# Batches of a group taken eight apart in a batched matrix product, with one store per group

## The chip, the cores and the metric

The kernel runs on one core of a Trainium2 chip. The core has five engines that take instructions on their own: PE (TensorE, matrix products), DVE (VectorE), ACT (ScalarE), POOL (GpSimd) and SP (SyncE, which here only waits and issues transfers). Data moves between the memory HBM and the on-chip buffer SBUF by DMA, over 16 DMA engines; matrix products land in PSUM, from which ACT and DVE copy them to SBUF. The time is the device time of one execution in microseconds; the kernel before takes 132.02 us (median of 3 runs, 131.93 to 132.05).

## The reference

```python
batch, dim_i, dim_j, dim_k = 32, 256, 512, 384
x: (batch, dim_i, dim_j) float32;  y: (batch, dim_j, dim_k) float32
out = np.einsum('bij,bjk->bik', x, y).astype(np.float32)
```

There are 32 independent products of a 256 x 512 by a 512 x 384 matrix. A batch of x has 512 KiB, of y 768 KiB, of out 384 KiB; 41.94 MB are read and 12.58 MB written.

## The kernel before

The 32 batches are worked on in `N` = 8 groups of `Q` = 4. The four batches of a group lie on the 128 partitions of SBUF side by side, 32 partitions (`PQ`) each. A partition holds 8 whole rows of x of its batch (16 KiB, one run in HBM), 16 rows of y (24 KiB, one run) and at the end 8 rows of out (12 KiB, one run). In the kernel before, a group is made of four neighbouring batches, so that partition p of the tile and the p-th run of the group in HBM go on evenly through all 128.

The four PE row groups of 32 each compute one of the four batches at the same time (`product`). The work on a group goes through the engines so:

- SP issues the loads into `x_sb` and `y_sb`, float32, two buffers each (`load_x`, `load_y`).
- POOL rounds them to float16, into `x_r` (two halves of a group, `NE`) and `y_r` (`round_x`, `round_y`; two or four pieces of y).
- DVE transposes x in blocks of 32 into `xt_sb` (`transpose_x`).
- PE accumulates over the 16 steps `t` into eight PSUM banks, one for each batch and half.
- ACT and DVE copy PSUM to `o_sb` (`collect`), which has room for all eight groups, so that no store has to be done before a later group is computed.
- SP issues the stores.

The order is written by hand, with semaphores. SP issues y(0), x(0), x(1), y(1) first. Then, for each group n from 2 on, x(n) follows when POOL has cast both halves of x(n-2), whose buffer it takes, and y(n) when the first half of x(n-1) has been cast, which POOL does after y(n-2). The stores stand behind all loads on SP: one of the groups 0 to 4 once group 5 is well on its way (`JOINED` = 5), one of 5 and 6 once group 7 is, and one of group 7 when ACT and DVE have copied it. A transfer adds 16 to its semaphore when it is done, and whoever uses the tile waits for 16.

Of the lines that the change touches, the source of a load and the target of a store are these:

```python
src = y[n * Q : (n + 1) * Q].rearrange("g (q t) k -> (g q) t k", t=T)
groups = out[first * Q : last * Q].rearrange("(n g) (s f) k -> (g s) n f k", g=Q, s=PQ)
```

## Time and profile before

| | |
|---|---|
| median of 3 runs | 132.02 us |
| the profiled execution, its own time | 132.13 us |
| its span, from the first to the last instruction | 130.8 us |
| bytes by the load and store queue | 54.53 MB |
| busy: PE / DVE / ACT / POOL | 47% / 63% / 64% / 57% of the span |
| mean granted TensorE clock | 0.823 |

The page cuts the span into 40 equal slices and gives for each the busy share in tenths (9 is 90% or more); the DMA row is the mean over the 16 DMA engines. A row of a queue has its packets, its megabytes and the time that the packets took as a share of 16 engines' span. A row of DMA issues has the kind of transfer, how many, the size of one, and the median time from issue to landing. In the table by stage each row is a stretch of the span, with the busy time and count of each engine, the granted clock, the DMA share and the GB/s. A row of waits says who waited for whom, how long in all and how often. L-numbers are lines of the kernel.

### The profile page before, as it was taken

Reading aid. Unit: us, or ns where it says so; the run is one execution under the profiler, and the core shown is the slowest. Engines: PE = TensorE matmul, PEld = TensorE weight load, DVE = VectorE, ACT = ScalarE, POOL = GpSimd, SP = SyncE. Lnnn points to the kernel's source line nnn. Section 1 sums busy time; section 2 is a strip of 40 time slices with the busy share of each in tenths; the row PEclk is TensorE's granted clock in tenths of the full one; section 3 lists DMA queues with packets and bytes.
Section 4 is the critical chain, followed back from the end, with each engine's and each line's share of the span. In section 5 each row is a group of like instructions: output and inputs, shape, how many; then the busy total and the mean of one; then the engine's idle time right before and its main releaser. Section 6 shows DMA issues by size and latency. Waiting matters only on the chain. (4 is left out here: it accounts for less than half of the span.)

```text
span 130.8 us, 3199 instructions
## 1 busy us (share of the span) xinstructions
PE 61.4 (47%) x1024; PEld 46.7 (36%) x1024; DVE 82.7 (63%) x144; ACT 84.1 (64%) x178; POOL 74.2 (57%) x42
## 2 busy tenths in 40 slices
PE   0000009910992589089329905980975499100000
PEld 0000009800991566046129604970953236000000
DVE  0000036899379999985997997599999957920000
ACT  0400000599659989993998899399999957994000
POOL 0006991199929965992899459758973970000000
PEclk9999999995589689977986985599599959965555
DMA  5999999999999999999999999999999999999995
GB/s 120 451 396 441 421 431 451 443 408 428 451 413 421 438 443 401 436 436 443 423 458 398 443 408 466 398 418 436 463 398 408 427 438 425 436 428 421 425 440 248
DMA packets 3379, 54.55 MB, mean 417 GB/s; under 512 B 304, under 2 KB 304, under 8 KB 304
## 3 DMA queue, kind: packets, MB, share of 16 engines
q1 hardware_dynamic: 3376, 54.53, 98.1%
q14 instruction: 3, 0.02, 0.0%
HBM read 41.94 MB, written 12.58 MB: 417 GB/s over the span
## 5 line engine op out<-in xcount | busy, mean ns | idle before, releaser
L165 ACT COPY o_sb<-o_ps (+1 forms) x176 | 82.6, 469 | 31.7 <-PE o_ps L217 29.6
L217 PE MATMUL o_ps<-y_r,xt_sb 32*128 32x384 f16 x1024 | 61.4, 384 | 50.4 <-PEq L214 49.5
L217 PEld LDWEIGHTS o_ps<-y_r,xt_sb 32*128 32x128 f16 x1024 | 46.7, 107 | 64.6 <-issue 56.8
L156 DVE STREAM_TRANSPOSE xt_sb<-x_r 128x256 f32<-128x256 f32 x64 | 38.1, 626 | 30.9 <-POOL x_r L126 18.4
L136 POOL CAST y_r<-y_sb 128x1536 f16<-128x1536 f32 (+1 forms) x22 | 44.3, 2049 | 15.8 <-DMA y_sb<-in_y_dram 15.3
L165 DVE COPY o_sb<-o_ps 32x384 f32 (+1 forms) x80 | 44.6, 557 | 1.6
L126 POOL CAST x_r<-x_sb 128x2048 f16<-128x2048 f32 x16 | 30.2, 1893 | 16.8 <-DVE o_sb L165 12.1
L202 ACT ACT_TABLE_LOAD x1 | 1.3, 1283 | 3.4 <-PEq L78 3.4
L265 POOL MEMSET const-float32-0.0<- 128x1 f32 x1 | 0.1, 98 | 0.2 <-issue 0.2
L202 ACT COPY spare<-const-float32-0.0 1x1 f32<-1x1 f32 x1 | 0.2, 190 | 0.0
L265 POOL MEMSET const-bfloat16-1.0<- 128x1 bf16 x1 | 0.1, 101 | 0.0
L265 POOL MEMSET const-uint8-127<- 128x1 uint8 x1 | 0.1, 101 | 0.0
L265 POOL MEMSET const-float32-1.0<- 128x1 f32 x1 | 0.1, 98 | 0.0
## 6 DMA issues: line engine op xcount, KB each, us to landing
y_sb<-in_y_dram SPq DMA_DIRECT2D x8, 3072.0 KB, 16.8
x_sb<-in_x_dram SPq DMA_DIRECT2D x8, 2048.0 KB, 17.0
out_dram<-o_sb SPq DMA_DIRECT2D x1, 7680.0 KB, 33.9
out_dram<-o_sb SPq DMA_DIRECT2D x1, 3072.0 KB, 17.3
out_dram<-o_sb SPq DMA_DIRECT2D x1, 1536.0 KB, 11.5
```

What stands on the lines that cost most here:

```text
L126: po.tensor_copy(x_r[:, e], x_sb[n % 2][:, e * H : (e + 1) * H]).then_inc(s_cast, 1)
L136: ins = po.tensor_copy(y_r[:, s], y_sb[n % 2][:, s])
L156: v.transpose(xt_w[:, w], words[:, e, w]).then_inc(s_xt, 1)
L165: ins = copy(o_sb[g * PQ : (g + 1) * PQ, n, e, h], o_ps[h * PQ : (h + 1) * PQ, e * Q + g, :K],)
L202: a_.copy(spare, nc.const_aps.tensor(0.0, [1, 1], F32))
L217: return te.add_instruction(mybir.InstMatmult(name=nc.get_next_instruction_name(), start_tensor_calc=start, stop_tensor_calc=stop, tile_si ...
L265: nc = _bacc.Bacc("TRN2", target_bir_lowering=False, num_devices=1)
```

## The change

Group n is now made of the batches n, n + 8, n + 16 and n + 24 (`x[n::N]`), where it had 4n to 4n + 3. The four batches of a group lie 8 batches apart in HBM: 4 MiB in x, 6 MiB in y, 3 MiB in out. Within a batch the 32 runs still follow each other without a gap. The pattern of the DRAM side of each transfer thus has the counts 4, 32 and a run, where it had 128 and a run; the SBUF side has 128 partitions as before. In place of three stores there are eight, one for each group, with the same pattern; they are issued at the same three points. The final wait is for the eight.

```diff
     def load_x(n):
-        src = x[n * Q : (n + 1) * Q].rearrange("g (p r) j -> (g p) r j", r=R)
+        src = x[n::N].rearrange("g (p r) j -> g p (r j)", r=R)
         return nc.sync.dma_start(out=x_sb[n % 2], in_=src).then_inc(s_x[n], 16)
 
     def load_y(n):
-        src = y[n * Q : (n + 1) * Q].rearrange("g (q t) k -> (g q) t k", t=T)
+        src = y[n::N].rearrange("g (q t) k -> g q (t k)", t=T)
         return nc.sync.dma_start(out=y_sb[n % 2], in_=src).then_inc(s_y[n], 16)
...
-    def store(first, last):
-        groups = out[first * Q : last * Q].rearrange("(n g) (s f) k -> (g s) n f k", g=Q, s=PQ)
-        src = o_sb[:, first:last].rearrange("p n e h k -> p n (e h) k")
-        sp.dma_start(out=groups, in_=src).then_inc(s_out, 16)
+    def store(n):
+        dst = out[n::N].rearrange("g (s f) k -> g s (f k)", s=PQ)
+        src = o_sb[:, n].rearrange("p e h k -> p (e h k)")
+        sp.dma_start(out=dst, in_=src).then_inc(s_out, 16)
...
-    sp.wait_ge(s_pe, chunk_done(JOINED, NE - 1, 0))
-    store(0, JOINED)
-    sp.wait_ge(s_pe, chunk_done(N - 1, NE - 1, 0))
-    store(JOINED, N - 1)
-    sp.wait_ge(s_act, NE)
-    sp.wait_ge(s_dve, NE)
-    store(N - 1, N)
+    for n in range(N):
+        if n == 0:
+            sp.wait_ge(s_pe, chunk_done(JOINED, NE - 1, 0))
+        elif n == JOINED:
+            sp.wait_ge(s_pe, chunk_done(N - 1, NE - 1, 0))
+        elif n == N - 1:
+            sp.wait_ge(s_act, NE)
+            sp.wait_ge(s_dve, NE)
+        store(n)
     sp.sem_inc(s_sp, 1)
-    sp.wait_op(s_out, 16 * 3, "sem-ge").then_inc(s_out, -16 * 3)
+    sp.wait_op(s_out, 16 * N, "sem-ge").then_inc(s_out, -16 * N)
```

## The prediction

> **What bounds the kernel now.** I read the page's slices first, then its queues, then the table by stage, the issues with their landings, and the chain of waits. The first lines are from the page of the kernel before.

> ```profile
> span 130.8 us, 3199 instructions
> ...
> DMA  5999999999999999999999999999999999999995
> ...
> DMA packets 3379, 54.55 MB, mean 417 GB/s; under 512 B 304, under 2 KB 304, under 8 KB 304
> ...
> q1 hardware_dynamic: 3376, 54.53, 98.1%
> ...
> HBM read 41.94 MB, written 12.58 MB: 417 GB/s over the span
> ...
> ACT 8%; PE 2%; issue 0%
> ```

> The DMA digits stand at 9 in every slice but the two ends, and the one queue fills all 16 DMA engines for 98.1% of the span. The chain of waits carries only 8% of ACT and 2% of PE, because it is followed through compute instructions and loses the trail where a transfer is what is late. So the bound is the movement of 54.53 MB, and no compute engine. The stages say it with rates; the columns that matter are the last two, the share of the 16 DMA engines and the GB/s.

> ```profile
> core 0: us, PE busy (x) PEld busy (x) DVE busy (x) ACT busy (x) POOL busy (x), PEclk, DMA share, GB/s
> 0.00:2.50 2.50, 0.00 (x0) 0.00 (x0) 0.00 (x0) 0.00 (x0) 0.20 (x4) 1.00 0.62 138
> 2.50:20.00 17.50, 0.62 (x7) 0.52 (x11) 1.56 (x3) 1.47 (x2) 9.13 (x6) 1.00 0.98 418
> 20.00:60.00 40.00, 26.04 (x439) 20.85 (x434) 33.32 (x59) 30.99 (x66) 29.47 (x14) 0.84 1.01 431
> 60.00:90.00 30.00, 18.75 (x332) 14.98 (x324) 25.65 (x46) 25.30 (x54) 21.29 (x10) 0.82 1.00 427
> 90.00:107.00 17.00, 11.24 (x176) 7.77 (x176) 15.30 (x27) 16.01 (x35) 14.04 (x10) 0.84 1.00 426
> 107.00:119.60 12.60, 4.74 (x88) 2.62 (x80) 6.86 (x12) 10.32 (x22) 0.03 (x1) 0.77 1.00 427
> 119.60:128.00 8.40, 0.00 (x0) 0.00 (x0) 0.00 (x0) 0.00 (x0) 0.00 (x0) 0.50 1.01 432
> 128.00:130.80 2.80, 0.00 (x0) 0.00 (x0) 0.00 (x0) 0.00 (x0) 0.00 (x0) 0.50 0.51 215
> ```

> From 20 us on, loads alone, loads beside stores and stores alone all run at 426 to 432 GB/s with every DMA engine busy. One DMA engine thus moves 427 / 16 = 26.7 GB/s, whichever way the bytes go. The bytes at that rate are 54.53 / 0.427 = 127.7 us; the other 3.1 us of the span are the start before the first bytes and the last landing. The profiled execution took 132.13 us, 1.33 beyond its span, and 0.11 above the median of 132.02; the sum below is made against 132.13.

> How a transfer is spread over the 16 engines can be read from the small packets: 304 of 3379 are under 512 B. The program has 8 loads of y, 8 of x and 3 stores (the issue rows below), and 304 / 19 = 16: one small packet from each of 16 engines for each transfer, its report to the semaphore. In all 19 transfers the outermost count of the pattern is 128, on the DRAM side as on the SBUF side.

> ```profile
> y_sb<-in_y_dram SPq DMA_DIRECT2D x8, 3072.0 KB, 16.8
> x_sb<-in_x_dram SPq DMA_DIRECT2D x8, 2048.0 KB, 17.0
> out_dram<-o_sb SPq DMA_DIRECT2D x1, 7680.0 KB, 33.9
> out_dram<-o_sb SPq DMA_DIRECT2D x1, 3072.0 KB, 17.3
> out_dram<-o_sb SPq DMA_DIRECT2D x1, 1536.0 KB, 11.5
> ```

> **The change part by part.** *Bytes and rows.* No byte is added or removed, and the contiguous runs are as long as before: 24 KB per partition for y, 16 KB for x, 12 KB for out. PE, DVE, ACT and POOL keep every instruction and every wait; only which batch sits in which partitions differs.

> *The pattern of the loads (the edit that decides).* Four neighbouring batches are one even walk: partition 32 follows partition 31 by the same step in DRAM, so 4 batches of 32 rows are one count of 128. With batches eight apart the step from row 31 to row 32 is another one, and the DRAM side has the counts 4, 32 and a run; the SBUF side keeps 128. Nothing in the trace of before shows a transfer with such a pattern, so its spread is bounded: 16 engines, if the hardware divides the 128 partitions as it does now, and 4, if it divides the outermost count, whose 4 entries can make no more than 4 shares. All rows at hand have 128 outermost, so they fit both ends. I take 4: a share has to be a plain pattern on both sides, and cutting the outermost count is the only cut that leaves each share one walk of 32 rows on both. [...]

> What 4 engines cost: an engine at 26.7 GB/s is taken to keep its rate, since it has kept it in all stages above (418 GB/s, with 0.98 of the engines, at the worst after 2.5 us). Then 4 x 26.7 = 106.8 GB/s, and 54.53 MB take 510.8 us instead of 127.7. With the same 3.1 us at the ends the span is 513.9, and with 1.3 beyond it the time is 515 us. At the 431 GB/s of the second long stage it would be 54.53 / 107.8 + 4.4 = 510; at the 418 of the first, 526.

> *The eight stores.* Each store has the same 4 x 32 pattern on the DRAM side and is in the sum above. Five issues are added on SP's queue.

> ```profile
> L96 SPq DMA_DIRECT2D out_dram<-o_sb x3: 345/390/403, 85.9 to 119.3; - x3
> L73 SPq DMA_DIRECT2D y_sb<-in_y_dram x8: 327/328/531, 0.7 to 84.1; - x8
> ```

> At 390 ns they are 2.0 us of SP. Groups 0 to 4 are stored at the one point where the first large store stood, and group 6 goes right behind group 5 at the point of the second, so no store waits for something new. They lie beside queued transfers; uncovered they would cost the 2.0 us. Whether the new pattern takes SP longer to issue is not to be seen in this trace: at the 531 ns of the slowest issue, against 328, all 24 issues would take 5 us more, also beside transfers.

> *Does the queue ever run dry?* With 107 GB/s a load of y lasts 3.146 / 0.107 = 29 us, a load of x 20 us, a group 49 us. The timeline of SP and of POOL shows how quickly the next issue follows.

> ```profile
> 20.27 0.33 SPq L69 DMA_DIRECT2D x_sb<-in_x_dram  x1
> ...
> 84.11 0.33 SPq L73 DMA_DIRECT2D y_sb<-in_y_dram  x1
> 85.85 33.76 SPq L96 DMA_DIRECT2D out_dram<-o_sb  x3
> ```

> ```profile
> 10.87 5.69 POOL L136 CAST y_r<-y_sb 128x1536 f16<-128x1536 f32 x4 [10.43 <-DMA y_sb<-in_y_dram]
> 16.51 3.73 POOL L126 CAST x_r<-x_sb 128x2048 f16<-128x2048 f32 x2
> ...
> 101.33 5.70 POOL L136 CAST y_r<-y_sb 128x1536 f16<-128x1536 f32 x4 [2.18 <-DMA y_sb<-in_y_dram]
> ```

> The load x(2) follows the last cast of x(0) at once (16.51 + 3.73 = 20.24, issued at 20.27). In the changed kernel, when x(0) has landed, x(1) and y(1) are still queued, 49 us of work against some 4 us of casts; later a buffer comes free with at least the 20 us of an x behind it. At the end, y(7) is in at 101.3 and the last store is issued at 119.3: 18 us of compute. Stores 0 to 4, queued behind y(7), cover it with 5 x 1.573 / 0.107 = 74 us. So the compute, which takes some 12 us a group, hides wholly, its waits on loads grow, and the sum stays at **515 us**.

> **The rivals.** *A: two engines share a way into SBUF.* Cut by batch, engine 0 writes partitions 0 to 31, engine 1 partitions 32 to 63, and so on, in the same order and nearly at the same time. If partitions 32 apart have one entrance of the width of one engine, each pair moves 26.7 GB/s together: 54.53 / 0.0534 = 1021, plus 4.4, 1026 us in full step, and less as one engine gets ahead; from a lead of one entrance on, nothing. The stages of before speak neither for nor against it: there 16 engines ran at once without loss, but between them they also covered all 128 partitions evenly. [...]

> *B: part of that, or the far-apart rows.* The four shares walk DRAM 4 MiB apart in x, 6 in y, 3 in out (8 batches each). If the x loads alone fell to half their rate, 16.8 MB would take 157 us more: 672. Against it speaks that only a quarter of the 427 GB/s is asked of HBM. [...] A pair in step for a part of the run ends here too, 560 to 900 us.

> *C: not slower.* The spread follows the 128 SBUF partitions, and all 16 engines stay at work. The time is then the same 127.7 us of bytes and 4.4 us around, 132.1; it hangs on the split alone. A gain of more than 0.3 us has no place to come from: the last store and its 11.5 us to landing stay.

> **How the numbers follow.** Forecast, four engines at full rate: 0.46, own range 507 to 545. A, mostly in step, 900 to 1030: 0.34. B, 560 to 900: 0.13. C: 0.07. The predicted time is 515. To leave out no more than 2 in 10 the range must take in A: 507 to 1030, which leaves out C and little else. Faster by over 0.2% is 0.03 (the sunny half of C), within 0.2% is 0.03, slower 0.94; 0.2% is about what a measurement of this kernel can tell from no change.

> **What would show it.** The row is from the waits of before.

> ```profile
> POOL y_r L136 <- DMA y_sb<-in_y_dram: 15.3, 5, 10.4
> ```

> Small packets: 24 transfers with 4 each are 96 under 512 B, against 384 if 16 engines report. The queue's share of 16 engines falls to about 25% and the rate to 107 GB/s; under A the rate is down to half of that with the share still near 25%, since a slowed engine is busy longer. The first load of y lands after some 31 us (29 of bytes and 2 of start), or some 60 under A. POOL's waits for y grow from 15.3 us in all to over a hundred. The prediction is wrong if the share stays near 98%, if the rate lies well under 107 GB/s, or if there are slices in which the queue is empty.

## The result, and the profile after

The changed kernel takes 545.41 us (median of 6 runs, 539.61 to 549.49) beside 131.99 us for the kernel before. The ratio is 4.1116, with a 95% interval of 4.0967 to 4.1266; it leaves out the two longest runs, 549.49 and 547.76, which count as slow because they lie more than 1.5% above the shortest. The forecast was 515 us with a range of 507 to 1030; the move is of the size that was forecast, and some 30 us are unexplained by the likeliest case.

The first lines are from the page of the changed kernel; the profiled execution is the longest one, 549.49 us.

```profile
span 548.1 us, 3204 instructions
...
DMA  2222222222222222222222222222222222222221
GB/s 50 56 59 64 77 96 108 91 88 103 107 113 108 105 105 108 109 108 108 108 109 108 108 106 109 110 108 105 106 105 109 106 108 108 108 108 108 108 108 69
DMA packets 3171, 54.55 MB, mean 100 GB/s; under 512 B 96, under 2 KB 96, under 8 KB 96
...
q1 hardware_dynamic: 3168, 54.53, 24.8%
```

The small packets are 96, which is 24 transfers with 4 reports each; the queue fills 24.8% of 16 engines, which is four engines without a pause. The DMA digit is 2 in all slices but the last: the queue did not run dry. But the GB/s row does not stand at 107 from the start. It begins at 50 and needs some six slices of 13.7 us to get there, with a second dip behind. By the row, 7.0 MB have moved after seven slices, and y(0), x(0) and x(1) are 7.34 MB together: the dip falls on the beginning of y(1). Why the rate drops again there was not tried. The table by stage of the same kernel puts numbers to it; the last two columns are the DMA share and the GB/s.

```profile
0.00:30.00 30.00, 0.00 (x0) 0.00 (x0) 0.00 (x0) 0.00 (x0) 0.20 (x4) 1.00 0.24 53
30.00:60.00 30.00, 0.00 (x0) 0.00 (x0) 0.00 (x0) 1.47 (x2) 2.23 (x2) 1.00 0.25 64
60.00:100.00 40.00, 7.38 (x128) 6.00 (x128) 7.57 (x13) 8.93 (x20) 7.19 (x5) 0.95 0.25 98
100.00:150.00 50.00, 8.49 (x128) 7.95 (x128) 9.75 (x17) 4.38 (x10) 9.17 (x4) 0.53 0.25 97
150.00:200.00 50.00, 8.09 (x128) 7.10 (x128) 10.93 (x20) 11.68 (x26) 9.17 (x4) 0.59 0.25 107
...
480.00:540.00 60.00, 0.00 (x0) 0.00 (x0) 0.00 (x0) 0.00 (x0) 0.00 (x0) 0.50 0.25 107
540.00:548.10 8.10, 0.00 (x0) 0.00 (x0) 0.00 (x0) 0.00 (x0) 0.00 (x0) 0.50 0.11 46
```

In the first 60 us the four engines are as busy as later (0.24 and 0.25) and move half to three fifths as much (53 and 64 GB/s). Against 107 GB/s the five stretches that fall short lose 15.1, 12.1, 3.4, 4.7 and, at the end, 4.6 us (each its length times the missing share of 107): 40 us. At 107 GB/s the bytes take 510 us, and 510 + 40 = 550 accounts for the span of 548. The last loss is that of the end: the DMA share falls to 0.11, as it would if the four engines, some us apart by then, do not end together.

Whom that hits first is seen in the timeline of SP and in the waits of the changed kernel.

```profile
0.73 0.71 SPq L73 DMA_DIRECT2D y_sb<-in_y_dram  x1
1.51 1.13 SPq L69 DMA_DIRECT2D x_sb<-in_x_dram  x2
2.68 48.37 SPq L73 DMA_DIRECT2D y_sb<-in_y_dram  x1
87.24 0.53 SPq L69 DMA_DIRECT2D x_sb<-in_x_dram  x1
104.97 0.53 SPq L73 DMA_DIRECT2D y_sb<-in_y_dram  x1
106.81 24.26 SPq L69 DMA_DIRECT2D x_sb<-in_x_dram  x1
```

```profile
POOL y_r L138 <- DMA y_sb<-in_y_dram: 109.9, 3, 57.3
...
ACT L204 <- PEq L78: 52.2, 1, 52.2
```

POOL waited 57.3 us for the first load of y. The issue of the fourth load held SP for 48.37 us, where most others took 0.5 to 0.7: that was not foreseen, and the start barrier at L78 waited with it (52.2 us on ACT). It was not the only one: the issues of x(3), x(5), x(6) and x(7), each behind loads that were still queued, held SP for 18.65 to 24.26 us. The DMA share of 0.25 beside them says that these holds cost nothing.

### The profile page after: what moved, and what is told of

Read it like the earlier page. It is cut to its first block, busy times and chain, and to the rows that moved or that the text cites. A ratio compares the mean times of both kernels' runs of the same rounds, so it can differ in the third digit from the quotient of the medians.

```text
span 548.1 us, 3204 instructions
## 1 busy us (share of the span) xinstructions
PE 63.6 (12%) x1024; PEld 53.8 (10%) x1024; DVE 82.7 (15%) x144; ACT 84.1 (15%) x178; POOL 74.3 (14%) x42
## 2 busy tenths in 40 slices
DMA packets 3171, 54.55 MB, mean 100 GB/s; under 512 B 96, under 2 KB 96, under 8 KB 96
## 3 DMA queue, kind: packets, MB, share of 16 engines
q1 hardware_dynamic: 3168, 54.53, 24.8%
HBM read 41.94 MB, written 12.58 MB: 99 GB/s over the span
## 5 line engine op out<-in xcount | busy, mean ns | idle before, releaser
L219 PE MATMUL o_ps<-y_r,xt_sb 32*128 32x384 f16 x1024 | 63.6, 401 | 378.2 <-PEq L216 378.2
L219 PEld LDWEIGHTS o_ps<-y_r,xt_sb 32*128 32x128 f16 x1024 | 53.8, 112 | 387.7 <-issue 382.9
L204 ACT ACT_TABLE_LOAD x1 | 1.3, 1283 | 52.2 <-PEq L78 52.2
## 6 DMA issues: line engine op xcount, KB each, us to landing
y_sb<-in_y_dram SPq DMA_DIRECT2D x8, 3072.0 KB
x_sb<-in_x_dram SPq DMA_DIRECT2D x8, 2048.0 KB
out_dram<-o_sb SPq DMA_DIRECT2D x8, 1536.0 KB
```

The costliest lines, as they stand in the source:

```text
L204: a_.copy(spare, nc.const_aps.tensor(0.0, [1, 1], F32))
L219: return te.add_instruction(mybir.InstMatmult(name=nc.get_next_instruction_name(), start_tensor_calc=start, stop_tensor_calc=stop, tile_si ...
```

## The experiments

Two things had to be told apart: that four engines are the bulk of the loss (theory S), and what makes the start slow. For that, theory P says that engines which write partitions 32 apart in step share one way into SBUF; rival H says that reads of HBM at such distances collide. All experiments are edits of the changed kernel. The kernels loads_far, stores_far, in_step, shares8, shares16, eight_close and eight_spread were run once each, the others four to eleven times; what is read from the single runs is far larger than the 1.8% by which the changed kernel's own runs spread.

**Loads alone, stores alone.** In the first, the stores of the kernel before are put back; in the second, its loads.

```diff
# loads_far: store(first, last), its waits and its three calls as in the kernel before
# stores_far:
-        src = x[n::N].rearrange("g (p r) j -> g p (r j)", r=R)
+        src = x[n * Q : (n + 1) * Q].rearrange("g (p r) j -> (g p) r j", r=R)
-        src = y[n::N].rearrange("g (q t) k -> g q (t k)", t=T)
+        src = y[n * Q : (n + 1) * Q].rearrange("g (q t) k -> (g q) t k", t=T)
```

> Only the loads have the 4 x 32 pattern; the three stores are those of the kernel before, so the products of the batches n, n+8, n+16, n+24 are put where 4n to 4n+3 belong. Theory S (a transfer runs on as many engines as its outermost count allows, loads and stores alike): engines 0 to 3 carry a quarter of 41.94 MB each and a sixteenth of 12.58 MB, 11.27 MB, which is 422 us at 26.7 GB/s; with 4.4 us at the ends 427, and with the slow start that the changed kernel shows in its first 60 us (about 27 us lost) some 455. Small packets: 16 x 4 + 3 x 16 = 112. Rival (only the stores are slow, the loads lose for another reason): far from it, under 300.

> Only the stores have the 4 x 32 pattern, eight of them; the loads are those of the kernel before, so the output's batches are put in other places. Theory S: loads 41.94 / 0.427 = 98 us, then the stores on four engines 12.58 / 0.1068 = 118 us, with 4.4 us at the ends 220 us; if two engines hold each other up at the start of the stores too, up to 30 more, 220 to 250. Small packets: 16 x 16 + 8 x 4 = 288. Rival (stores are spread by their SBUF side and lose nothing): 132.

Measured: 458.51 us with 112 small packets, and 222.40 us with 288. The GB/s rows of the two pages, loads_far first:

```profile
GB/s 49 56 62 62 68 90 108 106 94 92 92 102 110 107 108 106 109 110 105 108 106 111 105 110 105 110 108 108 109 106 186 423 232 108 105 98 106 106 313 171
```

```profile
GB/s 258 415 427 437 434 430 427 442 427 412 452 408 439 424 436 430 439 427 110 93 105 107 109 107 107 107 109 109 107 107 107 109 109 107 107 107 109 109 107 64
```

Theory S holds for each direction alone, and the slow start belongs to the loads: the far stores begin at 110 and go on at 107, but for one slice at 93. Between the two single edits, 326.5 us go to the loads (458.51 - 131.99) and 90.4 to the stores; their sum, 416.9, is close to the 413.4 of the whole change.

**The number of stores.** Loads of the kernel before, and eight stores of neighbouring batches.

```diff
-        dst = out[n::N].rearrange("g (s f) k -> g s (f k)", s=PQ)
+        dst = out[n * Q : (n + 1) * Q].rearrange("g (s f) k -> (g s) (f k)", s=PQ)
# and the sources of load_x and load_y as in stores_far
```

> Eight stores, one for each group, with the four neighbouring batches of the kernel before, so that every pattern has 128 outermost. Theory S: the number of stores costs nothing but 5 issues of SP beside queued transfers: 132.0, within 0.3 us. Rival (the number of stores is part of the loss, by about 2 us of fixed cost each): 134 to 142. Small packets: 24 x 16 = 384.

Measured: 132.06 us, ratio 1.0006 (0.9997 to 1.0015). Eight stores in place of three cost nothing that can be seen; at the rival's 2 us each the five more would have cost 10.

**Another distance.** Batches two apart in place of eight.

```diff
-        src = x[n::N]...
+        src = x[n // 2 * 8 + n % 2 : n // 2 * 8 + n % 2 + 7 : 2]...
# the same for y and out
```

> The same 4 x 32 patterns, but the four batches of a group lie two apart instead of eight: 1 MiB in x, 1.5 MiB in y, 0.75 MiB in out. Theory P (the slow start comes from two engines that write partitions 32 apart in step and share a way into SBUF; the distance in HBM does not matter): the same time as with eight apart, 538 to 550, and again half the rate in the first 30 us. Rival H (the slow start comes from HBM addresses a large power of two apart): the start runs at 107 GB/s, 512 to 520.

Measured: 546.33 us (545.15 to 550.65). From its page:

```profile
GB/s 50 55 59 60 73 94 107 92 91 99 109 108 107 107 109 108 107 107 109 109 106 107 109 108 105 110 109 106 110 106 106 106 107 108 107 107 108 107 107 70
```

The start is the same, with its second dip. So it is not the distance of 4, 6 and 3 MiB that makes it slow; that any distance in HBM does, 1 MiB in x and 1.5 MiB in y as well, is not excluded by this run alone.

**A head start.** Engines 0 to 2 get something to do before y(0).

```diff
+    pad = sbuf("pad", [81, 2000], F32)
...
+    rows = x[0].rearrange("(p r) j -> p (r j)", r=4)
+    nc.sync.dma_start(out=pad[64:81], in_=rows[:17, :2000]).then_inc(s_out, 16)
+    nc.sync.dma_start(out=pad[:51], in_=rows[:51, :2000]).then_inc(s_out, 16)
     # then y(0), x(0), x(1), y(1) as before
```

> The changed kernel, with two small loads ahead of y(0) into a tile that nothing reads: one of 17 rows of 8 KB, which engine 0 alone takes, and one of 51 rows, 17 each for engines 0, 1 and 2. [...] Theory P: full rate, 107 GB/s, as soon as all four are at work; engine 0 has 0.27 MB more to move, 10 us: 515 + 10 = 525. Rival H, or any other cause that comes with the start (cold addresses, the DMA engines warming up): the slow start stays, 545 + 10 = 555.

Measured: 521.31 us (521.16 to 521.44), 24.1 below the changed kernel although 0.54 MB more are moved. There are 100 small packets, four more than in the changed kernel: one for the load of 17 rows and three for that of 51. The table by stage of this run:

```profile
0.00:30.00 30.00, 0.00 (x0) 0.00 (x0) 0.00 (x0) 0.00 (x0) 0.20 (x4) 1.00 0.23 95
30.00:60.00 30.00, 0.00 (x0) 0.00 (x0) 0.00 (x0) 1.47 (x2) 5.70 (x4) 1.00 0.25 106
60.00:100.00 40.00, 8.22 (x128) 7.73 (x128) 12.56 (x22) 10.33 (x22) 7.46 (x4) 0.73 0.25 109
100.00:150.00 50.00, 7.62 (x128) 7.07 (x128) 10.35 (x18) 10.32 (x22) 9.17 (x4) 0.57 0.25 108
```

53 and 64 GB/s have become 95 and 106, and the dip from 100 to 150 us is gone. So the slow start does not come with the start of the program as such; it goes when the engines are set apart in time.

**Back in step.** From x(2) on each load waits for the one before it.

```diff
     for n in range(2, N):
         sp.wait_ge(s_cast, NE * (n - 1))
+        sp.wait_ge(s_y[n - 1], 16)
         load_x(n)
         sp.wait_ge(s_cast, NE * (n - 1) + 1)
+        sp.wait_ge(s_x[n], 16)
         load_y(n)
```

> The changed kernel, but from x(2) on SP waits until a load has landed before it issues the next, so that the four engines start each load together again. Theory P (engines in step share, and need some 60 us to get out of step): each load of y takes about 50 to 55 us and each of x 35 to 38, against 29 and 20; a group 85 to 93, plus 2 us of start for each of 12 loads; with the stores 820 to 960 in all. Rival (only the very start of the program is slow): 545 + 12 x 2 to 3 = 570 to 580.

Measured: 795.79 us. SP's timeline in this run gives the time of a load as the distance of two issues:

```profile
135.46 0.53 SPq L69 DMA_DIRECT2D x_sb<-in_x_dram  x1
169.97 0.53 SPq L73 DMA_DIRECT2D y_sb<-in_y_dram  x1
223.25 0.53 SPq L69 DMA_DIRECT2D x_sb<-in_x_dram  x1
257.73 0.53 SPq L73 DMA_DIRECT2D y_sb<-in_y_dram  x1
...
589.51 0.53 SPq L69 DMA_DIRECT2D x_sb<-in_x_dram  x1
```

A load of x takes 34.5 us, one of y 53.3, and all later ones 34 to 37 and 54 to 57, against 20 and 29 at 107 GB/s. Those are the times that theory P gave for a load. The total came out 24 us below the expected 820 to 960. Eight groups at 85 us, 24 us of starts and 118 us of stores make 822, the lower end; but the edit leaves the first two groups as they were, and they were in after 135 us. From there on five groups took 454 us (135.46 to 589.51), 91 us each, as expected with the starts. The 2 us of a start are the author's estimate; what the run shows is a DMA share of 0.23 from 120 to 500 us, where four engines without a pause make 0.25. The last stage, stores alone, has 107 GB/s:

```profile
700.00:790.00 90.00, 0.00 (x0) 0.00 (x0) 0.00 (x0) 0.00 (x0) 0.00 (x0) 0.50 0.25 107
```

**More engines.** The outermost count is 8 and 16.

```diff
+M = 2   # shares8; 4 in shares16
-        src = x[n::N].rearrange("g (p r) j -> g p (r j)", r=R)
+        src = x[n // M :: N // M].rearrange("g (p r) j -> g p (r j)", r=R)[:, PQ // M * (n % M) : PQ // M * (n % M + 1)]
# the same for y and out
```

> A dose: the outermost count is 8, from 8 batches with 16 partitions each (the rows that meet in a product are then of different batches, so the output is not the reference's; bytes, runs and instructions are the same). Theory S: 8 engines, 54.53 / (8 x 0.0267) = 255 us, with 4.4 at the ends 260, and with a slow start as with 4 engines 275 to 295. Small packets: 24 x 8 = 192. Rival (the pattern is slow for another reason than the number of engines, such as three dimensions): as with 4, some 545.

> The same with an outermost count of 16, from 16 batches with 8 partitions each (the output is not the reference's for the same reason). Theory S with P: all 16 engines work, but engines four apart take partitions 32 apart at the same time, so it starts at about half the rate and gets faster as they fall out of step: 145 to 175. Theory S with H (distances in HBM, which are smaller here, 1 to 1.5 MiB): 132 to 140, at full rate from the start. Small packets: 24 x 16 = 384.

Measured: 419.58 us with 192 small packets, and 234.72 us with 384. Both counts are those of theory S. Both times missed what was expected of it: 419.58 us lies far above 275 to 295, though below the rival's 545, and 234.72 above 145 to 175. From the page of shares8, then from the table by stage of shares16:

```profile
GB/s 94 110 103 113 113 110 116 108 110 109 113 113 113 105 113 114 118 108 119 126 115 118 114 125 130 118 127 128 129 132 130 144 123 135 186 213 215 213 216 180
```

```profile
20.00:60.00 40.00, 10.82 (x170) 9.43 (x174) 13.44 (x24) 10.35 (x22) 17.42 (x10) 0.77 1.01 213
...
150.00:200.00 50.00, 16.84 (x256) 14.62 (x256) 20.67 (x36) 20.69 (x44) 18.62 (x10) 0.64 1.00 211
200.00:233.00 33.00, 8.50 (x128) 6.38 (x128) 8.14 (x14) 10.34 (x22) 5.71 (x4) 0.60 0.92 379
```

With 16 engines busy all the time (1.00), the loads stay at half of 427 for 200 us; in shares8 they begin at 94 to 113, half of what eight free engines move, and creep up. In shares16 the stores behind the loads bring the last stage to 379. Read under P, the engines did not get out of step here within the 200 us, as four had done; the expectation had carried over the 60 us of the changed kernel. Why the half rate lasts longer with more engines was not tried. One thing that the edit changes is on record: of each transfer an engine walks 32 partitions when there are four engines, 16 with eight and 8 with sixteen; whether that is the reason stays open.

**One batch at a time.** Each transfer is cut into four of one batch, first in the order 0, 1, 2, 3, then 0, 2, 1, 3.

```diff
     def load_x(n):
-        src = x[n::N].rearrange("g (p r) j -> g p (r j)", r=R)
-        return nc.sync.dma_start(out=x_sb[n % 2], in_=src).then_inc(s_x[n], 16)
+        for g in (0, 1, 2, 3):   # (0, 2, 1, 3) in batch_loads_alt
+            src = x[n + g * N].rearrange("(p r) j -> p (r j)", r=R)
+            dst = x_sb[n % 2][g * PQ : (g + 1) * PQ].rearrange("p r j -> p (r j)")
+            nc.sync.dma_start(out=dst, in_=src).then_inc(s_x[n], 16)
# the same for y and out; POOL waits for 16 * Q, the end for 16 * N * Q
```

> Batches eight apart as in the change, but every load and every store is cut into four transfers, one for each batch, each with 32 rows that lie one after the other in HBM and 32 partitions, in the order of the batches 0, 1, 2, 3. Theory S: the outermost count is 32, so all 16 engines work, two rows each. [...] Rival H (the distance in HBM between engines is the cause; here they read neighbouring rows): 132 to 136. Small packets: 96 x 16 = 1536.

> The same in the order of the batches 0, 2, 1, 3, so that transfers into partitions under 64 and from 64 on take turns. [...] Rival H: no difference between the two orders.

Measured: 235.60 us (235.47 to 235.68) and 227.71 (227.36 to 227.95), with 1536 small packets each. From the page of batch_loads:

```profile
GB/s 176 206 200 210 221 210 228 206 204 199 224 202 202 210 216 227 218 190 231 206 206 206 213 230 202 204 199 224 202 202 223 221 216 203 329 367 403 420 428 241
```

The batches are the ones of the change, all 16 engines work, HBM is read in neighbouring rows, and from the second slice on the loads run at 190 to 231 GB/s up to the slice in which the stores begin. The cutting itself is not the cause: the stores are cut in the same way and reach 428 GB/s. The order is worth 8 us. Rival H, which expected 132 to 136 us, has no place for either. But the forecasts under P were missed as well, 150 to 200 us for the one and 135 to 170 for the other: they had the rate rise in the course of the run, and as in shares16 the loads stayed at about half rate to the end, for which 260 had been expected. What sets the gain of the second order no run shows.

**The same HBM side, two SBUF sides.** The transfers of the kernel before are cut into 16 of eight runs.

```diff
+    def where(i):
+        return slice(8 * i, 8 * i + 8)                                        # eight_close
+        return slice(i // 4 * 32 + i % 4, i // 4 * 32 + i % 4 + 29, 4)        # eight_spread
     def load_x(n):
+        src = x[n * Q : (n + 1) * Q].rearrange("g (p r) j -> (g p) (r j)", r=R)
+        dst = x_sb[n % 2].rearrange("p r j -> p (r j)")
+        for i in range(16):
+            nc.sync.dma_start(out=dst[where(i)], in_=src[8 * i : 8 * i + 8]).then_inc(s_x[n], 16)
# the same for y and out
```

> Every transfer of the kernel before (four neighbouring batches) is cut into 16 of eight runs that lie one after the other in HBM, which eight engines take, one run each. Here the eight runs go to eight partitions side by side, 8i to 8i + 7. [...] Between 400 and 1026 us, far above eight_spread. Rival H (the loss is on the HBM side): the same as eight_spread.

> The same transfers with the same HBM side, but the eight runs of a transfer go to eight partitions four apart within 32 (the rows of y are then at other places than the multiplication expects, so the output is not the reference's). Theory P: the eight engines use eight different ways, 8 x 26.7 = 213 GB/s from the start: 54.53 / 0.2136 + 4.4 = 260 us, some more for 384 transfers. Rival H: the same as eight_close. For the stores, which read SBUF: if reading shares the ways too, their packets of 12 KB are as slow in eight_close as the loads are; if only writing does, they keep 460 ns in both.

Measured: 359.33 us and 271.63. From the pages, eight_close first:

```profile
GB/s 66 66 66 71 69 92 106 112 106 122 104 110 103 147 134 121 126 152 176 143 146 201 178 173 177 196 201 209 221 202 211 208 189 203 214 210 210 217 209 135
```

```profile
DMA  3445555344544554555454545545454555555433
GB/s 127 211 212 213 213 218 222 135 136 173 206 211 211 216 222 210 213 215 222 206 224 207 216 210 221 215 207 213 211 224 200 209 213 215 209 211 215 182 153 131
```

## Why the prediction was right, and where it was off

*The split.* Right. That the outermost count of 4 leaves four engines was argued from the shape of the pattern, and no run had shown it; the 96 small packets and 24.8% show it, and 8, 16 and 32 as outermost count gave 8, 16 and 16 reports a transfer (192 and 384 for 24 transfers, 1536 for 96). The reason given, that a share has to be a plain pattern on both sides, was the author's estimate; the runs show the counts and not why a transfer is cut so. Case C, 16 engines and 132 us, is out.

*The rate of one engine.* This is the term that was mis-sized. "An engine at 26.7 GB/s is taken to keep its rate": it does from 150 us on (107 GB/s for four), and in the first 60 us it has half to three fifths (53 and 64). The sum of 515 lacked some 30 us of it. So the time came out 0.4 us above the own range of the forecast, 507 to 545, by a part of rival A; that it lies well inside the whole range is owed to the range having been opened to 1030 for A. One of the prediction's own signs of being wrong, a rate well under 107 GB/s, was there for the first five slices (50 to 77).

*Rival A.* Right in the rate at the start and wrong in its duration. The engines begin at 53 GB/s together, about the halves that it named, and the first load of y comes after 57 us against "some 60 under A"; but four engines are at the full rate after 70 to 80 us (the sixth and seventh slice, 96 and 108 GB/s) and, but for the second dip, stay there, and A's 900 to 1030 needed them to stay at the half. Where they start every load together, 796 us come out; where they are set apart in time, the first 30 us run at 95 GB/s. That the cause is one entrance for partitions 32 apart fits these runs and is not shown by one of them alone. What is shown of other partitions: the loads of batch_loads, 16 engines into 32 neighbouring partitions, run at 190 to 231 GB/s, about half of 427, and eight_spread, eight engines into partitions four apart, at the full rate of eight engines, 213 GB/s.

*Rival B.* The distance of eight batches in HBM is out: two apart took 546.33 us, with the same start. What B said of "a pair in step for a part of the run" fits what happened, half to three fifths of the rate for 60 us (53 and 64 GB/s), at a smaller price than its 560.

*The stores.* Right: eight cost nothing beside three (132.06 us), and their pattern costs what four engines take (222.40 alone, 220 expected).

*The queue.* Right in its result: the DMA share is 0.24 to 0.25 in every stage but the last. Wrong in the price of an issue: 531 ns was the upper bound, and the fourth load's issue took 48.37 us, four later ones 18.65 to 24.26. All of them lay beside transfers that were still moving, the cover that the prediction had named for issues of half a microsecond.

*The end.* The 74 us of stores covered the last group's compute, as written: from 480 to 540 us no engine but the DMA works. The 4.6 us lost in the last stretch were in the sum only as a part of its 3.1 us for both ends.

## What to carry to other kernels

Before regrouping the batches of a load, look whether the pattern in HBM still goes through all 128 partitions in one step: with an outermost count of 4 the transfers here had 4 engines (24.8% of 16), though their runs are 12 to 24 KB long, and the count of small packets in the profile says so at once. Sixteen engines were not enough here where a transfer wrote 32 neighbouring partitions (190 to 231 GB/s in batch_loads), or engines four apart wrote partitions 32 apart at the same time (211 to 213 in shares16): look at GB/s beside the DMA share, since a busy share of 1.00 at half of 427 GB/s was here the sign of engines that hold each other up. Cutting each transfer of 128 partitions into four of 32 took 235.60 us, where transfers of 128 partitions with the same bytes take 132.

## What the runs showed of the hardware that was not expected

- The slow start does not last with four engines (96 and 108 GB/s after 70 to 80 us) and does with 16 (211 to 213 GB/s, half the rate, through 200 us in shares16). What drives engines apart, if that is what ends it, and why it takes longer with more of them, stays open.
- The loss was seen in loads only. In in_step the stores went at 107 GB/s behind loads at 56 to 64 (120 to 500 us), in batch_loads at up to 428 GB/s, and stores_far lost at most one slice at 93 GB/s. In shares16 the last loads and the first stores are only some 3 us apart:

```profile
190.00:198.00 8.00, 0.00 (x0) 0.00 (x0) 3.70 (x7) 4.94 (x11) 0.52 (x1) 0.61 1.01 212
201.00:206.00 5.00, 2.48 (x31) 2.26 (x32) 0.59 (x1) 0.00 (x0) 4.40 (x4) 0.50 1.02 433
```

  Loads at half the rate are followed at once by stores at the full rate, which speaks against the engines having been apart by then (from 206 to 213 us the stores fall to 379 GB/s for a reason that is not known). That reading SBUF has no such limit was not tried by an experiment of its own.
- SP can be held by an issue: 48.37 us for the fourth load in the changed kernel, which has 32 runs for each of four engines. In shares8, which has 16 runs for each of eight engines, ACT waited 4.6 us at the start barrier behind the same four issues, against 52.2. In the kernel before, a store with 40 runs for each of 16 engines was issued in at most 0.40 us beside queued loads. That the hold goes with how many runs stand queued for an engine is the author's estimate from these three cases; the limit was not looked for.
- The changed kernel's own runs spread over 1.8% (539.61 to 549.49), the kernel with the head start over 0.05%. That the spread is the luck of how soon the engines part is argued from this, not shown; it would explain the two longest runs too.
